# RWKV keys first with one norm chain and one block order for both heads, and an inverse with aligned diagonal blocks, in a two-layer hybrid decoder trunk

## The chip, the cores and the metric

The kernel runs on one core of a Trainium2 chip. The metric is the device time of one execution in microseconds, as the median of several runs. The engines are TensorE (matmuls, PE in the rows; its weight loads are PEld), VectorE (DVE), ScalarE (ACT), GpSimd (POOL) and the DMA queues (SP issues them).

## What is computed

Two layers, each on 512 tokens of width 1024, all in float32:

```python
h = rms_norm(x); p = h @ w_in             # columns for MLA, RWKV-7, Mamba-2 and three gates
x = x + (sum_i sigmoid(g_i) * (o_i @ W_br_i)) @ W_out
x = x + relu(rms_norm(x) @ W_1)**2 @ W_2
# the RWKV branch, 8 heads of 64:
p = p + (token_shift(p) - p) * mu;  r, k, v, xw, xa, xg = split(p)
decay = exp(-exp(-softplus(-(w0 + tanh(xw) @ w2)) - 0.5));  a = sigmoid(a0 + xa @ a2)
kk = k * k_k;  kk = kk / max(norm_per_head(kk), 1e-12);  k = k * (1 + (a - 1) * k_a)
state = state * decay + (state @ -kk) (kk * a)^T + v k^T;  y = state @ r     # per token
y = group_norm(y) + sum(r * k * r_k) * v;  o = y * (sigmoid(xg) @ g2)
```

The kernel computes the recurrence in 8 chunks of 64 tokens: within a chunk the delta rule becomes a triangular system, whose inverse is formed explicitly.

## The kernel before

Activations lie with features on the partitions: a tile of 128 x 512 holds two heads. A projection (`proj`, line 256 in `mm3`) is 24 matmuls of 128 x 512 (8 slices of the depth, three products of high and low parts); its weights are brought by DMA as `wraw`, rounded by ScalarE to `wH` (L222), and VectorE forms the rest `wL` (L223).

`rwkv_prep` loops over four blocks i of two heads each. For each it projects and mixes r, k (and v in layer 1; layer 2 has done v ahead with a residual) in `shifted` (L306, L358, L359). It forms the decay (`lw`, the scan at L437, `c`, `E1`), `a` (L450, L451), the squares `sq` and their sums per token and head `ss` (L454, L457), a reciprocal root by Newton steps on 8 columns (L200 to L208), a spread copy of it (L461), transposes to bring it back (`inv`, L464), and the normalised `kk` (L466). Then it writes the tiles `AR` (-kk and r, times decay; L471, L473) and `BK` (kk*a and k, over decay; L480, L481), each with an axis of two halves. The two heads of a tile, partitions 0 to 63 and 64 to 127, have these halves in opposite order, so each product is made in two pieces of 64 partitions, the second of most pairs on GpSimd. Then come the bonus `rk` (L484), its sum `bo` (L486), transposes of v (`vT`), and `N`, the 64 x 64 products of BK and AR for 8 chunks and two heads (L503), masked into `NA` (L505).

`rwkv_inverse` inverts 64 triangular blocks of 64 x 64 in `NA`. The two 32 x 32 diagonal blocks lie at columns 0 to 31 for the upper 32 rows and 32 to 63 for the lower, so the block transposes into `NT` (L627), back from `X` (L641) and into `T1` (L646) go over 32 partitions each, 4, 4 and 2 of them. Between them stand 31 steps of two VectorE operations (L635, L637). Small matmuls `Q` (L652) and `X12` (L661, the tile `X` in the rows) make the off-diagonal block.

`rwkv_chain` runs over the 8 chunks: `prepare` makes `A` (L545, both halves of BK against both of AR), the masked `CW` and `LT` (L549 to L563); then `RY` (L576), `U` (L585, with NA) and `YS` (L598) advance the state.

The stages are emitted with others interleaved (`mixer`): after blocks 2 and 3 of `rwkv_prep` (`PF`) and at the yields of the inverse and the chain (`FILL`) one step of MLA's projections or one gate projection is emitted. The source order is a priority only: when the program is built, a planner with estimated costs fixes the order on each engine and puts in the waits, so an engine can run later work earlier. Buffers limit it: two PSUM banks for projections, three of the tag `r`, eight SBUF tiles `pg`.

## Time and profile before

| what | us |
|---|---|
| median of 3 runs (2192.79 to 2195.28) | 2192.87 |
| the profiled execution | 2201.93 |
| its span, first to last instruction | 2199.8 |
| TensorE busy (mean granted clock 0.98) | 2114.2 |
| VectorE busy | 1421.7 |
| ScalarE busy | 911.9 |
| GpSimd busy | 359.8 |

The rows below come from the profiled execution. Busy time of TensorE is modelled, and its small matmuls overlap each other, so pace is read from a group of them. In the timeline a row can gather several instructions of a kind (xN); its time goes from the first one's start to the last one's end. A mean granted clock of 1.00 is 2.4 GHz, 0.50 is 1.2 GHz. The key stages lie at about 36 to 147 us (layer 1) and 1115 to 1248 us (layer 2), the inverses behind them to about 223 and 1322 us.

### The profile page before, as it was taken

Reading aid. Unit: us, or ns where it says so; the run is one execution under the profiler, and the core shown is the slowest. Engines: PE = TensorE matmul, PEld = TensorE weight load, DVE = VectorE, ACT = ScalarE, POOL = GpSimd, SP = SyncE. Lnnn points to the kernel's source line nnn. Section 1 sums busy time; section 2 is a strip of 40 time slices with the busy share of each in tenths; the row PEclk is TensorE's granted clock in tenths of the full one; section 3 lists DMA queues with packets and bytes.
Section 4 is the critical chain, followed back from the end, with each engine's and each line's share of the span. In section 5 each row is a group of like instructions: output and inputs, shape, how many; then the busy total and the mean of one; then the engine's idle time right before and its main releaser. Section 6 shows DMA issues by size and latency. Waiting matters only on the chain. (4 is left out here: it accounts for less than half of the span.)

```text
span 2199.8 us, 29935 instructions
## 1 busy us (share of the span) xinstructions
PE 2114.2 (96%) x11592; PEld 1672.0 (76%) x11592; DVE 1421.7 (65%) x2394; ACT 911.9 (41%) x1568; POOL 359.8 (16%) x258
## 2 busy tenths in 40 slices
PE   7998999999999999999998889999999999999999
PEld 6667767667778888888876677676677788888887
DVE  7988777977756543443569978779777554444433
ACT  5343433764423443333433434337644234433332
POOL 1120020111322111111021200202113121111110
PEclk9998999999999999999999979999999999999999
DMA  5332233114364233333432222331143642333232
GB/s 193 91 95 69 71 113 127 44 58 148 125 216 134 89 106 96 96 96 96 139 98 77 82 70 74 108 124 42 65 146 121 217 133 87 105 96 96 96 96 96
DMA packets 95613, 232.61 MB, mean 106 GB/s; under 512 B 17744, under 2 KB 27088, under 8 KB 95472
## 3 DMA queue, kind: packets, MB, share of 16 engines
q1 hardware_dynamic: 95472, 230.71, 33.0%
q8 instruction: 91, 1.49, 0.3%
q14 instruction: 50, 0.41, 0.1%
HBM read 197.64 MB, written 33.03 MB: 105 GB/s over the span
## 5 line engine op out<-in xcount | busy, mean ns | idle before, releaser
L256 PE MATMUL pj<-hH,wH 128*128 128x512 f32 (+1 forms) x1536 | 616.8, 402 | 8.4 <-ACT hH L225 8.4
L256 PE MATMUL pj<-hH,wL 128*128 128x512 f32 (+1 forms) x1536 | 616.7, 401 | 0.9 <-DVE wL L223 0.9
L256 PE MATMUL pj<-hL,wH 128*128 128x512 f32 (+1 forms) x1536 | 615.5, 401 | 0.1
L222 ACT CAST wH<-wraw 128x1024 fp32r<-128x1024 f32 (+1 forms) x314 | 327.6, 1043 | 654.4 <-PE pj L256 317.9
L223 DVE TENSOR_TENSOR wL<-wraw,wH 128x1024 fp32r<-128x1024 f32 (+1 forms) x314 | 415.2, 1324 | 140.1 <-ACT wH L222 139.6
L256 PEld LDWEIGHTS pj<-hH,wH 128*128 128x128 f32 (+1 forms) x1536 | 292.1, 190 | 75.2 <-ACT hH L225 8.4
L256 PEld LDWEIGHTS pj<-hH,wL 128*128 128x128 f32 (+1 forms) x1536 | 291.2, 190 | 65.7 <-issue 4.0
L256 PEld LDWEIGHTS pj<-hL,wH 128*128 128x128 f32 (+1 forms) x1536 | 291.9, 190 | 63.8 <-issue 2.5
L256 PE MATMUL pf<-uH,wH 128*128 128x512 f32 x512 | 199.2, 389 | 0.0
L256 PE MATMUL pf<-uL,wH 128*128 128x512 f32 x512 | 199.2, 389 | 0.0
L256 PE MATMUL pf<-uH,wL 128*128 128x512 f32 x512 | 199.2, 389 | 0.0
L324 POOL TENSOR_TENSOR u<-u,rsb 128x512 f32<-128x512 f32 x64 | 111.3, 1741 | 496.4 <-ACT u L323 474.7
L339 DVE TENSOR_TENSOR x<-x,pf 128x512 f32<-128x512 f32 x128 | 88.1, 688 | 139.0 <-PE pf L256 136.9
L223 DVE TENSOR_TENSOR uL<-u,uH 128x512 fp32r<-128x512 f32 x64 | 44.1, 692 | 138.1 <-ACT uH L222 138.1
L256 PEld LDWEIGHTS pf<-uH,wH 128*128 128x128 f32 x512 | 96.1, 188 | 20.1
L256 PEld LDWEIGHTS pf<-uL,wH 128*128 128x128 f32 x512 | 96.1, 188 | 20.0
L256 PEld LDWEIGHTS pf<-uH,wL 128*128 128x128 f32 x512 | 96.1, 188 | 19.8
L977 POOL TENSOR_TENSOR E<-E,CB 128x1280 f32<-128x1280 f32 x16 | 49.4, 3088 | 377.3 <-ACT E L974 333.6
L256 PE MATMUL br<-oH,wH 128*128 128x512 f32 x256 | 102.9, 403 | 6.3 <-ACT oH L222 6.3
L256 PE MATMUL br<-oL,wH 128*128 128x512 f32 x256 | 103.2, 403 | 3.0 <-DVE oL L223 3.0
L256 PE MATMUL br<-oH,wL 128*128 128x512 f32 x256 | 102.3, 400 | 0.0
L326 ACT ACTIVATE u<-u 128x512 f32<-128x512 f32 x64 | 40.5, 633 | 118.9 <-POOL u L324 118.9
(363 smaller groups left out, 2972.4 us busy)
## 6 DMA issues: line engine op xcount, KB each, us to landing
wraw<-in_w SPq DMA_DIRECT2D x302, 512.0 KB, 3.6
gd<-gt SPq DMA_DIRECT2D x48, 256.0 KB, 2.1
th<-gd SPq DMA_DIRECT2D x16, 512.0 KB, 3.9
xd<-x SPq DMA_DIRECT2D x8, 512.0 KB, 5.2
o_ssm<-ys SPq DMA_DIRECT2D x16, 256.0 KB, 2.1
x<-xd SPq DMA_DIRECT2D x8, 512.0 KB, 5.9
of<-o_ssm SPq DMA_DIRECT2D x16, 256.0 KB, 4.4
t<-gd SPq DMA_DIRECT2D x16, 256.0 KB, 2.7
```

What stands on the lines that cost most here:

```text
L222: nc.scalar.copy(out=H, in_=src)
L223: nc.vector.tensor_tensor(out=Lo, in0=src, in1=H.bitcast(F32), op=ALU.subtract)
L256: nc.tensor.matmul(out=ps, lhsT=ww if w_is_lhs else aa, rhs=aa if w_is_lhs else ww, start=first and k == 0 and q == 0, stop=last and k == ...
L324: nc.gpsimd.tensor_tensor(out=u, in0=u, in1=self.rsb, op=ALU.mult)
L326: nc.scalar.activation(out=u2, in_=u, func=AF.Square)
L339: nc.vector.tensor_tensor(out=xk, in0=xk, in1=ps, op=ALU.add)
L977: eng.tensor_tensor(out=e, in0=e, in1=CB[g], op=ALU.mult)
```

## The change

In `rwkv_prep` the four k blocks are projected first (`key`), straight into `BK[:, i, :, 1, :]`, and their sums of squares share one PSUM bank; one reciprocal root on 32 columns serves all. The decay of block i + 1 (`decay`) is emitted within block i. r is projected straight into `AR[:, i, :, 1, :]`. The spread copy of the root moves to ScalarE. Both heads have the same order of halves, so each product of AR and BK is one VectorE operation on 128 partitions, and GpSimd has none; the halving in `a` is folded into the factors. `pg` has 6 tiles for 8, `c` and `E1` have two each for one.
`N` is formed in 32-wide pieces, so that each diagonal block of 32 x 32 lies at columns 0 to 31 of its own rows: in `rwkv_inverse` one transpose of 128 partitions stands for each group of 4 or 2. Then the lower diagonal blocks are copied to columns 32 to 63 by ScalarE and their old place is cleared by GpSimd. `A` is formed in pieces of 64 x 64, with the halves reversed for the second head, so that CW has the order it had; `LT` takes three copies for two. Layer 1's norm projects block 4 ahead in place of block 0. The scaled parameters `dv[:, 26:30]`, `dv[:, 40:48]` and the paddings are changed to suit.

```diff
-        pg = lambda name: tp.tile([P, S], F32, name=name, tag="pg", bufs=8)
+        pg = lambda name: tp.tile([P, S], F32, name=name, tag="pg", bufs=6)
...
+            for d in range(2):
+                p = slice(64 * hp + 32 * d, 64 * hp + 32 * d + 32)
+                nc.gpsimd.affine_select(out=self.mst[p, 0, 0:32], in_=self.mst[p, 0, 0:32], pattern=[[1, 32]],
+                                        compare_op=ALU.is_gt, fill=0.0, base=0, channel_multiplier=-1)
+            nc.vector.memset(self.mst[64 * hp + 32:64 * hp + 64, 0, 32:64], 0.0)
+            for t, q, strict in ((self.msk, 1 - hp, True), (self.msk, hp, False)):
                 nc.gpsimd.affine_select(out=t[h, q, :], in_=t[h, q, :], pattern=[[1, 64]],
...
@@ -355,14 +364,15 @@
         st = self.sh[self.shn % 2]
         self.shn += 1
         self.scaled(st[:, 3:S + 3], ps)
-        nc.scalar.activation(out=out, in_=st[:, 3:S + 3], func=AF.Identity, scale=self.dv[:, j:j + 1])
-        nc.vector.scalar_tensor_tensor(out=out, in0=st[:, 2:S + 2], scalar=self.pc("rwkv_mu", j), in1=out, op0=ALU.mult,
-                                       op1=ALU.add)
+        v = (lambda t: t) if len(out.shape) == 2 else lambda t: t.rearrange("p (c t) -> p c t", c=8)
+        nc.scalar.activation(out=out, in_=v(st[:, 3:S + 3]), func=AF.Identity, scale=self.dv[:, j:j + 1])
+        nc.vector.scalar_tensor_tensor(out=out, in0=v(st[:, 2:S + 2]), scalar=self.pc("rwkv_mu", j), in1=out,
+                                       op0=ALU.mult, op1=ALU.add)
 
...
-        for i in range(4):
-            r, k = pg("r"), pg("k")
-            self.shifted(i, r)
+        pss = PS("ss")
+        def key(i):
+            k = BK[:, i, :, 1, :]
             self.shifted(4 + i, k)
-            if l == 0:
-                v = T("v", [P, S], 4)
-                self.shifted(8 + i, v)
-                nc.sync.dma_start(out=self.vfirst[i], in_=v)
-            else:
-                v = vs[i]
+            sq = pg("sq")
+            nc.scalar.activation(out=v8(sq), in_=k, func=AF.Square, scale=self.pc("rwkv_k_k", i))
+            for q in range(NC4):
+                nc.tensor.matmul(out=pss[:, 8 * i + 2 * q:8 * i + 2 * q + 2], lhsT=sq[:, q * P:(q + 1) * P],
+                                 rhs=self.bones[:, 0:P:64], start=True, stop=True)
+        def decay(i):
 
             ps = PS("lw")
             nc.tensor.matmul(out=ps, lhsT=self.wa2[0:64, i * P:(i + 1) * P], rhs=xwa[0:64], start=True, stop=True)
@@ -431,9 +444,11 @@
             nc.tensor.matmul(out=pa, lhsT=self.wa2[64:128, i * P:(i + 1) * P], rhs=xwa[64:128], start=True, stop=True)
             t = lw[:, :, 1:65]
             nc.scalar.activation(out=t, in_=v8(ps), func=AF.Tanh, scale=0.5, bias=self.dv[:, 14 + i:15 + i])
+            th = pg("a")
+            nc.scalar.activation(out=th, in_=pa, func=AF.Tanh, scale=0.5, bias=self.dv[:, 18 + i:19 + i])
             nc.vector.tensor_scalar(out=t, in0=t, scalar1=-0.5 * INV_SQRT_E,
                                     scalar2=-0.5 * INV_SQRT_E, op0=ALU.mult, op1=ALU.add)
-            c = T("c", [P, 8, 65])
+            c = T("c", [P, 8, 65], 2)
             nc.vector.tensor_tensor_scan(out=fl(c), data0=fl(scanm), data1=fl(lw), initial=0.0, op0=ALU.mult,
                                          op1=ALU.add)
             m = T("m", [P, 8], 2)
@@ -442,49 +457,54 @@
                                     op=ALU.subtract)
             nc.vector.tensor_tensor(out=f[:, i, 0:7], in0=c[:, 0:7, 64], in1=m[:, 1:8], op=ALU.add)
             nc.scalar.activation(out=f[:, i, 0:7], in_=f[:, i, 0:7], func=AF.Exp)
-            E1 = T("E1", [P, 8, 65])
+            E1 = T("E1", [P, 8, 65], 2)
             nc.scalar.activation(out=E1, in_=c, func=AF.Exp)
             nc.scalar.activation(out=c, in_=c, func=AF.Exp, scale=-1.0)
-            a = pg("a")
-            nc.scalar.activation(out=a, in_=pa, func=AF.Tanh, scale=0.5, bias=self.dv[:, 18 + i:19 + i])
-            nc.vector.tensor_scalar(out=a, in0=a, scalar1=0.5, scalar2=0.5, op0=ALU.mult, op1=ALU.add)
-            sq = pg("sq")
-            nc.scalar.activation(out=sq, in_=k, func=AF.Square, scale=self.pc("rwkv_k_k", i))
-            ps = PS("ss")
-            for q in range(NC4):
-                nc.tensor.matmul(out=ps[:, 2 * q:2 * q + 2], lhsT=sq[:, q * P:(q + 1) * P], rhs=self.bones[:, 0:P:64],
-                                 start=True, stop=True)
-            inv = self.rsqrt(tp, ps[:, 0:8], [P, 8], 1.0, 0.0, "kk", lo=1e-24)
-            ib = sq
-            nc.vector.tensor_copy(out=v8(ib), in_=inv.rearrange("p (g o) -> p g o", o=1).to_broadcast([P, 8, 64]))
+            return th, c, E1
+        key(0)
+        key(1)
+        dec = decay(0)
+        key(2)
+        key(3)
+        inv = self.rsqrt(tp, pss[:, 0:32], [P, 32], 1.0, 0.0, "kk", lo=1e-24)
+        for i in range(4):
+            r, k = AR[:, i, :, 1, :], BK[:, i, :, 1, :]
+            self.shifted(i, r)
+            if l == 0:
+                v = T("v", [P, S], 4)
+                self.shifted(8 + i, v)
+                nc.sync.dma_start(out=self.vfirst[i], in_=v)
+            else:
+                v = vs[i]
+            th, c, E1 = dec
+            kk = pg("kk")
+            nc.scalar.copy(out=v8(kk), in_=inv[:, 8 * i:8 * i + 8].rearrange("p (g o) -> p g o", o=1).to_broadcast([P, 8, 64]))
             ps = PS("inv")
             for q in range(NC4):
-                nc.tensor.transpose(out=ps[:, q * P:(q + 1) * P], in_=ib[:, q * P:(q + 1) * P], identity=self.ident)
-            kk = sq
-            nc.vector.scalar_tensor_tensor(out=kk, in0=k, scalar=self.pc("rwkv_k_k", i), in1=ps, op0=ALU.mult,
+                nc.tensor.transpose(out=ps[:, q * P:(q + 1) * P], in_=kk[:, q * P:(q + 1) * P], identity=self.ident)
+            nc.vector.scalar_tensor_tensor(out=v8(kk), in0=k, scalar=self.dv[:, 44 + i:45 + i], in1=v8(ps), op0=ALU.mult,
                                            op1=ALU.mult)
 
-            for hp in range(2):
-                h, e = half(hp), nc.gpsimd if hp else nc.vector
-                nc.vector.scalar_tensor_tensor(out=AR[h, i, :, hp, :], in0=v8(kk)[h], scalar=-1.0, in1=E1[h, :, 0:64],
-                                               op0=ALU.mult, op1=ALU.mult)
-                e.tensor_tensor(out=AR[h, i, :, 1 - hp, :], in0=v8(r)[h], in1=E1[h, :, 1:65], op=ALU.mult)
-            nc.vector.tensor_tensor(out=kk, in0=kk, in1=a, op=ALU.mult)
-            nc.vector.tensor_scalar(out=a, in0=a, scalar1=self.pc("rwkv_k_a", i), scalar2=self.dv[:, 26 + i:27 + i],
+            nc.vector.scalar_tensor_tensor(out=AR[:, i, :, 0, :], in0=v8(kk), scalar=-2.0, in1=E1[:, :, 0:64],
+                                           op0=ALU.mult, op1=ALU.mult)
+            nc.vector.scalar_tensor_tensor(out=kk, in0=th, scalar=1.0, in1=kk, op0=ALU.add, op1=ALU.mult)
+            nc.vector.tensor_tensor(out=BK[:, i, :, 0, :], in0=v8(kk), in1=c[:, :, 1:65], op=ALU.mult)
+            nc.vector.tensor_scalar(out=th, in0=th, scalar1=self.dv[:, 40 + i:41 + i], scalar2=self.dv[:, 26 + i:27 + i],
                                     op0=ALU.mult, op1=ALU.add)
-            nc.vector.tensor_tensor(out=k, in0=k, in1=a, op=ALU.mult)
-            for hp in range(2):
-                h, e = half(hp), nc.gpsimd if hp else nc.vector
-                e.tensor_tensor(out=BK[h, i, :, hp, :], in0=v8(kk)[h], in1=c[h, :, 1:65], op=ALU.mult)
-                e.tensor_tensor(out=BK[h, i, :, 1 - hp, :], in0=v8(k)[h], in1=c[h, :, 1:65], op=ALU.mult)
-            rk = r
-            nc.vector.scalar_tensor_tensor(out=rk, in0=r, scalar=self.pc("rwkv_r_k", i), in1=k, op0=ALU.mult, op1=ALU.mult)
+            nc.vector.tensor_tensor(out=k, in0=k, in1=v8(th), op=ALU.mult)
+            rk = kk
+            nc.vector.scalar_tensor_tensor(out=v8(rk), in0=r, scalar=self.pc("rwkv_r_k", i), in1=k, op0=ALU.mult,
+                                           op1=ALU.mult)
+            nc.vector.tensor_tensor(out=r, in0=r, in1=E1[:, :, 1:65], op=ALU.mult)
+            nc.vector.tensor_tensor(out=k, in0=k, in1=c[:, :, 1:65], op=ALU.mult)
+            if i < 3:
+                dec = decay(i + 1)
             ps = PS("bo")
             nc.tensor.matmul(out=ps, lhsT=self.bones, rhs=rk, start=True, stop=True)
-            bo = r
+            bo = rk
             nc.vector.tensor_tensor(out=bo, in0=v, in1=ps, op=ALU.mult)
             for hp in range(2):
                 nc.sync.dma_start(out=self.bod[i - i % 2 + hp, half(i % 2)], in_=bo[half(hp)])
@@ -500,8 +520,11 @@
             ps = PS("N")
             for q in range(8):
                 for hp in range(2):
-                    nc.tensor.matmul(out=ps[half(hp), q * 64:q * 64 + 64], lhsT=BK[half(hp), i, q, hp, :],
-                                     rhs=AR[half(hp), i, q, hp, :], start=True, stop=True)
+                    for d in range(2):
+                        o = 64 * hp + 32 * d
+                        a = AR[half(hp), i, q, 0, :].rearrange("p (u t) -> p u t", u=2)
+                        nc.tensor.matmul(out=ps[o:o + 32, q * 64:q * 64 + 64], lhsT=BK[half(hp), i, q, 0, 32 * d:32 * d + 32],
+                                         rhs=a[:, ::-1] if d else a, start=True, stop=True)
             nc.vector.tensor_tensor(out=NA[:, 8 * i:8 * i + 8, :], in0=v8(ps), in1=self.mst.to_broadcast([P, 8, 64]),
                                     op=ALU.mult)
             yield i
@@ -542,11 +565,14 @@
             for i in range(4):
                 for hp in range(2):
                     h = half(hp)
-                    nc.tensor.matmul(out=pss[hp][:, i * P:(i + 1) * P], lhsT=BK[h, i, c].rearrange("p a t -> p (a t)"),
-                                     rhs=AR[h, i, c].rearrange("p a t -> p (a t)"), start=True, stop=True)
+                    rhs = AR[h, i, c, ::-1] if hp else AR[h, i, c].rearrange("p a t -> p (a t)")
+                    for a in range(2):
+                        nc.tensor.matmul(out=pss[hp][half(a), i * P:(i + 1) * P], lhsT=BK[h, i, c, 1 - a if hp else a, :],
+                                         rhs=rhs, start=True, stop=True)
             for hp in range(2):
                 h, o, ps = half(hp), half(1 - hp), pss[hp]
-                nc.scalar.copy(out=CW[h, hp], in_=AR[h, :, c].rearrange("p i a t -> p i (a t)"))
+                src = AR[h, :, c, ::-1] if hp else AR[h, :, c]
+                nc.scalar.copy(out=CW[h, hp].rearrange("p i (a t) -> p i a t", a=2), in_=src)
                 pv = ps.rearrange("p (i n) -> p i n", i=4)
                 mk = self.msk[o].rearrange("p (o a) t -> p o (a t)", o=1).to_broadcast([64, 4, P])
                 nc.vector.tensor_tensor(out=CW[o, hp], in0=pv[o], in1=mk, op=ALU.mult)
@@ -559,8 +585,9 @@
                     nc.tensor.transpose(out=pt[:, i * P:(i + 1) * P], in_=BK[:, i, c].rearrange("p a t -> p (a t)"),
                                         identity=self.ident)
                 pv = pt.rearrange("p (i n) -> p i n", i=4)
+                nc.scalar.copy(out=LT[:, 0, :, half(0)], in_=pv[:, :, half(0)])
                 for hp in range(2):
-                    nc.scalar.copy(out=LT[:, hp, :, half(hp)], in_=pv[:, :, half(hp)])
+                    nc.scalar.copy(out=LT[half(1 - hp), 1, :, half(1)], in_=pv[half(hp), :, half(1)])
 
         Sk = None
         prepare(0)
@@ -619,12 +646,11 @@
 
     def rwkv_inverse(self, p4, PS, NA):
 
         nc = self.nc
         b3 = lambda t: t.rearrange("p (s t) -> p s t", s=32)
-        blk = [(32 * d, slice(64 * hp + 32 * d, 64 * hp + 32 * d + 32)) for hp in range(2) for d in range(2)]
         NT, Xf, tmp = b3(p4("NT")), p4("X"), b3(p4("Xt"))
-        for d, p in blk:
-            nc.vector.transpose(out=NT[p], in_=NA[p, :, d:d + 32].rearrange("p b t -> p t b"))
+        nc.vector.transpose(out=NT, in_=NA[:, :, 0:32].rearrange("p b t -> p t b"))
         yield 2
         X = b3(Xf)
         nc.gpsimd.memset(Xf, 0.0)
@@ -637,13 +663,14 @@
             nc.vector.tensor_tensor(out=X[:, 0:t, t:32], in0=X[:, 0:t, t:32], in1=tt, op=ALU.add)
             if t % 8 == 0:
                 yield 1
-        for d, p in blk:
-            nc.vector.transpose(out=NA[p, :, d:d + 32].rearrange("p b t -> p t b"), in_=X[p].rearrange("p s t -> p t s"))
+        nc.vector.transpose(out=NA[:, :, 0:32].rearrange("p b t -> p t b"), in_=X.rearrange("p s t -> p t s"))
         yield 1
         T1, Q = b3(p4("T1")), b3(p4("Q"))
+        nc.vector.transpose(out=T1, in_=NA[:, :, 0:32])
         for hp in range(2):
-            s1 = slice(64 * hp, 64 * hp + 32)
-            nc.vector.transpose(out=T1[s1], in_=NA[s1, :, 0:32])
+            s2 = slice(64 * hp + 32, 64 * hp + 64)
+            nc.scalar.copy(out=NA[s2, :, 32:64], in_=NA[s2, :, 0:32])
+            nc.gpsimd.memset(NA[s2, :, 0:32], 0.0)
         for g in range(2):
             ps = PS("Q")
             for b in range(16):
...
```

## Rows read from the trace of the kernel before

**Rows 1.** The page's engines: busy us (share of the span) and instructions.

```profile
PE 2114.2 (96%) x11592; PEld 1672.0 (76%) x11592; DVE 1421.7 (65%) x2394; ACT 911.9 (41%) x1568; POOL 359.8 (16%) x258
```

**Rows 2.** Windows, engine busy us (instructions): plain projections, and the key stage.

```profile
825.00:850.00 25.00, 25.00 (x112) 20.67 (x112) 11.64 (x13) 9.87 (x14) 5.36 (x3) 1.00 0.30 88
1200.00:1225.00 25.00, 22.30 (x131) 16.55 (x130) 22.67 (x45) 8.86 (x15) 3.89 (x3) 1.00 0.31 93
```

**Rows 3.** TensorE's waits over the whole span: total us, times, longest us.

```profile
PE Q L652 <- DVE T L646: 10.1, 2, 5.2
...
PE bo L486 <- DVE r L484: 8.1, 6, 1.9
PE inv L464 <- DVE sq L461: 7.3, 7, 1.9
...
PE up L256 <- DVE cL L226: 5.1, 2, 2.6
...
PE ss L457 <- ACT sq L454: 2.9, 7, 1.6
```

**Rows 4.** VectorE's groups, 1150 to 1250 us: busy us, mean ns, idle before.

```profile
L223 DVE TENSOR_TENSOR wL<-wraw,wH 128x1024 fp32r<-128x1024 f32 (+1 forms) x11 | 12.7, 1153 | 0.2 <-ACT wH L222 0.2
L471 DVE SCALAR_TENSOR_TENSOR AR<-sq,E 64x512 f32<-64x512 f32 x8 | 5.5, 685 | 0.2
...
L437 DVE TENSOR_TENSOR_SCAN c<-scanm,lw 128x520 f32<-128x520 f32 x4 | 5.0, 1240 | 0.3
L484 DVE SCALAR_TENSOR_TENSOR r<-r,prm,k 128x512 f32<-128x512 f32 x4 | 4.9, 1229 | 0.0
L480 DVE TENSOR_TENSOR BK<-sq,c 64x512 f32<-64x512 f32 x4 | 4.7, 1182 | 0.0
...
L207 DVE TENSOR_TENSOR rskk<-rskk 128x8 f32<-128x8 f32 x12 | 3.7, 306 | 0.3
```

**Rows 5.** Timeline of VectorE and GpSimd in layer 1: start us, us, instruction.

```profile
59.08 1.68 DVE L480 TENSOR_TENSOR BK<-sq,c 64x512 f32<-64x512 f32 x1
...
58.73 1.49 POOL L480 TENSOR_TENSOR BK<-sq,c 64x512 f32<-64x512 f32 x1 [6.51 <-DVE sq L474]
```

**Rows 6.** Tile NA: duration ns min/median/max, first and last start us.

```profile
L505 DVE TENSOR_TENSOR NA<-N,mst x8: 683/692/692, 66.6 to 1246.4; 128x512 f32<-128x512 f32 x8
L627 DVE STREAM_TRANSPOSE NT<-NA x8: 1929/2000/2060, 148.5 to 1253.2; 32x1024 f32<-32x1024 f32 x8
L641 DVE STREAM_TRANSPOSE NA<-X x8: 2168/2270/2352, 198.3 to 1304.1; 32x1024 f32<-32x1024 f32 x8
...
L646 DVE STREAM_TRANSPOSE T<-NA x4: 1233/1234/1236, 207.5 to 1307.5; 32x1024 f32<-32x1024 f32 x4
```

**Rows 7.** Windows as in rows 2; the granted clock is third from the end.

```profile
208.00:224.00 16.00, 15.26 (x292) 11.97 (x294) 7.38 (x8) 6.67 (x11) 0.00 (x0) 0.57 0.27 85
...
180.00:190.00 10.00, 8.55 (x44) 8.15 (x45) 7.93 (x21) 2.45 (x5) 1.27 (x1) 0.66 0.18 54
1276.00:1288.00 12.00, 10.31 (x47) 9.77 (x48) 8.87 (x22) 3.08 (x7) 1.27 (x1) 0.57 0.13 45
1232.00:1240.00 8.00, 7.70 (x32) 6.20 (x33) 6.14 (x11) 1.04 (x1) 2.10 (x1) 0.57 0.07 8
```

**Rows 8.** Timeline of TensorE: start us, us, instruction, tile rows*columns, x records.

```profile
63.88 1.12 PE L486 MATMUL bo<-r,bones 128*128 128x512 f32 x2 [1.33 <-DVE r L484]
...
65.38 1.15 PE L503 MATMUL N<-AR,BK 64*64 64x64 f32 x32
...
222.23 0.40 PE L576 MATMUL RY<-Z,CW 128*64 128x64 f32 x6
222.56 1.19 PE L661 MATMUL X<-NA,Q 32*32 32x32 f32 x62
...
247.52 1.16 PE L545 MATMUL A<-AR,BK 64*128 64x128 f32 x16
...
249.20 0.98 PE L576 MATMUL RY<-Z,CW 128*64 128x64 f32 x26
```

More of the change, by code (lines that the diff above doesn't have):

```diff
@@ L98, in setup @@
             h = slice(64 * hp, 64 * hp + 64)
-            for t, q, strict in ((self.mst, 0, True), (self.msk, 1 - hp, True), (self.msk, hp, False)):
+            for d in range(2):
[4 more added lines that the diff above has]
+            for t, q, strict in ((self.msk, 1 - hp, True), (self.msk, hp, False)):
                 nc.gpsimd.affine_select(out=t[h, q, :], in_=t[h, q, :], pattern=[[1, 64]],
@@ L158, in load_params @@
         self.prm = prm
-        dv = self.par.tile([P, 40], F32, name="dv", tag="dv", bufs=1)
+        dv = self.par.tile([P, 56], F32, name="dv", tag="dv", bufs=1)
         self.dv = dv
@@ L171, in load_params @@
                                     scalar2=None, op0=ALU.mult)
-        nc.vector.tensor_scalar(out=dv[:, 26:30], in0=prm[:, cs["rwkv_k_a"]:cs["rwkv_k_a"] + 4], scalar1=-1.0,
+        nc.vector.tensor_scalar(out=dv[:, 26:30], in0=prm[:, cs["rwkv_k_a"]:cs["rwkv_k_a"] + 4], scalar1=-0.5,
                                 scalar2=1.0, op0=ALU.mult, op1=ALU.add)
+        for o, n in ((40, "rwkv_k_a"), (44, "rwkv_k_k")):
+            nc.vector.tensor_scalar(out=dv[:, o:o + 4], in0=prm[:, cs[n]:cs[n] + 4], scalar1=0.5, scalar2=None,
+                                    op0=ALU.mult)
         self.hg = prm[:, cs["q_rope_g"]:cs["q_rope_g"] + 64].rearrange("p (a d) -> p a d", a=2)
@@ L1117, in run @@
                 ns, npool = self.open("nm")
-                self.norm(x, "norm_mix_g", npool, first, [B_RW + j for j in ((12, 13, 8) if l else (12, 13, 0))])
+                self.norm(x, "norm_mix_g", npool, first, [B_RW + j for j in ((12, 13, 8) if l else (12, 13, 4))])
                 ns.close()
@@ L1138, in mixer @@
         mc_s, mcp = self.open("mc", "right")
-        self.pad(mqp, 736)
+        self.pad(mqp, 672)
         qT = mqp.tile([P, NC4, 768], F32, name="qT", tag="qT", bufs=1)
@@ L1192, in mixer @@
         self.gp = mgp
-        self.pad(mgp, 864)
+        self.pad(mgp, 800)
         m = mgp.tile([P, KD, S], F32, name="m", tag="m", bufs=1)
```

## The prediction

> **What bounds the kernel now.** I read the page's table of engines first: TensorE is busy for 2114.2 of 2199.8 us [rows 1]. No other engine comes near, so a time can only be won where TensorE stands still, does less, or runs at its lower clock. Next the windows. A stretch of plain projections shows TensorE busy for all of 25.00 us with 112 matmuls, so a matmul of 512 columns starts every 0.22 us and a projection of 24 takes 5.4 us. In the key stage (`rwkv_prep`), TensorE is busy for 22.30 us and VectorE for 22.67 us of 25 [rows 2]: both are nearly full, and each waits for the other in turn. The list of TensorE's waits tells for what: 10.1 us (2 times) for the last transposes of the inverse, 8.1 us for the bonus product `r`, 7.3 us for the spread norm `sq`, 5.1 us for the low half `cL` of an MLA projection (queued on VectorE between operations of the inverse), 2.9 us for the squares [rows 3]. Last the granted clock: it drops behind several of these waits. In 208 to 224 us, behind the wait for the transposes, its mean is 0.57; 0.66 and 0.57 behind the two waits for `cL`, 0.57 around one for the spread norm [rows 7]. The clock there is at the lower of its two levels, 1.2 GHz in place of 2.4, for most of the stretch, and busy time at 1.2 GHz is half lost. The second layer's wait for the transposes has the same pattern.
>
> **What the planner does.** The order on an engine is not the source order: `RY` of the chain started before `X` of the inverse, though it is emitted after it [rows 8]. So a matmul that follows its own producer in the source doesn't make TensorE stand still by itself; the planner puts other projections ahead. TensorE waits where an operation on the chip lasts longer than it was planned. That is how I read every wait in rows 3, and it decides what I expect of the order with keys first.
>
> **The parts.**
>
> *VectorE in the key stage.* From the groups of layer 2 (four blocks) [rows 4]: the two half-height `AR` products become one of full height: half of 5.5, 2.8 us less. That full height costs no more than half height is shown by 692 ns for 128x512 (`NA<-N,mst`) [rows 6] beside 685 ns for the 64x512 of `AR` [rows 4]. One chain of the norm with 32 columns in place of four with 8: for its dearest line three quarters of 3.7, 2.8 us less. `BK` and `rk` get longer while GpSimd works: the `BK` product took 1.68 us while GpSimd's lasted from 58.73 to 60.22 us [rows 5], against 0.69 us undisturbed. Without GpSimd's half, `BK` falls from 4.7 to 4 x 0.69 = 2.8 us (1.9 less) and `rk` from 4.9 to 4 x 0.73 (2.0 less). That is 9.5 us of VectorE's time in a layer from four groups alone, with further small ones (the halving of `a`, the spread copy, which goes to ScalarE) on top. ScalarE was the less busy engine and gets eight copies of some 0.6 us: I cost them at nothing; planned by themselves, with the norm ready long before, nothing waits for them but the first.
> What ends later than planned today (`r` behind GpSimd's lock, `sq` behind the norm chain) is what goes: 8.1 + 7.3 = 15.4 us of TensorE's waits. The new order will have its own misses, so I keep a third of them: **10 us gained**, bounds 0 and 15.4.
>
> *The inverse.* Four transposes of 2.00 us become one, four of 2.27 one, two of 1.23 one [rows 6]: 3 x 2.00 + 3 x 2.27 + 1.23 = 14.0 us of VectorE's queue in a layer, taking a transpose of 128 partitions to last as long as one of 32 (not shown for this operation; by the heights above). Two copies and two memsets of `NA` are added, on ScalarE and GpSimd, beside the transpose of `T1`; the first Q matmul needs neither, the X matmuls need the copies, U the memset. The waits of 10.1 us lie behind six of these transposes (4 x 2.27 + 2 x 1.23 = 11.5 us, then 2.27 + 1.23 = 3.5); a planning error in proportion leaves 3 us: **7 us gained**, bounds 0 and 10.1. For `cL`, which queues behind the first four, I take **3 us** of 5.1, bounds 0 and 5.1. TensorE has filling work enough when the chain starts earlier, since the gates that follow in the chain are emitted as before.
>
> *The clock.* The lost time is (1 - clock) x stretch: 0.43 x 16 = 6.9 us, twice with layer 2; 0.34 x 10 = 3.4; 0.43 x 12 = 5.2; 0.43 x 8 = 3.4 [rows 7]; together 25.8 us. With about half of the waits in front gone, I take half: **13 us gained**, bounds 0 and 25.8.
>
> *TensorE's own work.* `N` has 64 records for 32 in a block, `A` 32 for 16 in a chunk, with tiles of half the width. Before, `N` needs (1.15 - 0.22) / 31 = 30 ns for a record, `A` (1.16 - 0.27) / 15 = 59 ns, `RY` (0.98 - 0.22) / 25 = 30 ns, `X` (1.19 - 0.24) / 61 = 16 ns [rows 8] (the first record's own length, 0.22 to 0.27 us, is taken off). `RY` alternates two column halves on the same rows, `A` two row halves on the same columns, and both go at the faster pace. If all four quadrants run together, a record of half width costs half: nothing added. If just two do, `A` doubles: + 0.89 x 16 chunks = 14.2 us, and `N` + 0.93 x 8 blocks = 7.4 us. I take `A` at 0, for it combines what `RY` and `A` show singly, and `N` at **3 us lost**, since its records come near the 16 ns of `X`; bounds 0 and 21.6.
> `RY`'s weights are loaded for the column half that the matmul before doesn't use, on the same rows, without a gap in its pace of 30 ns [rows 8]. The Trainium skill ("TensorE: Matmul & The Clock Gate", Part 3: Packing small matmuls) says the contrary for this kind of order: a weight load overlaps a running matmul only when the row group differs. By that rule the new `A` and `N`, which issue the two column parts of one row group in succession, would pair badly; what it would give is rival B, and `RY`'s row speaks against it.
>
> *Other edits.* The masks, the scaled parameters and the padding touch no busy stretch: nothing. `pg` falls from 8 to 6 buffers, and one of three PSUM banks `r` is held by `pss` while the keys run; the projections of the keys cover that with 5.4 us each: nothing, and some 3 us (as the squares' waits of rows 3) if not.
>
> **Sum.** 10 + 7 + 3 + 13 - 3 = 30 us less. The profiled execution took 2201.9 us (span 2199.8): 2172. The median of the runs shown stands to it as 2192.87 to 2201.93, which gives **2163 us**. All gains and no cost: 15.4 + 10.1 + 5.1 + 25.8 = 56.4 less, 2137.
>
> **Rivals.**
> *B, quadrants run in pairs only.* 21.6 us for `A` and `N` in place of 3: 33 - 21.6 = 11 less, 2190 for the execution, **2182**. For it: no row shows four parts at once. Against: both pairs do run together.
> *C, keys first takes the cover away, slower.* Today a block has two projections on TensorE beside its VectorE work; afterwards all keys come first, and a block in layer 2 keeps one. VectorE's work for a block is then at most 1.2 (`wL`) + 1.4 (`sh`, mix) + 3.2 (decay: the scan of 1.24, two of 0.7, two small ones of 0.3) + 6.3 (nine products of 0.7) + 1.4 (bonus, mask) = 13.5 us, an estimate that puts every full-width operation without a row at 0.7 [rows 4, 6]. TensorE's is 5.4 + 1.15 (`N`) + 1.1 (`bo`) + some 2.5 (decay matmuls and transposes, an estimate at the pace of `bo`) = 10.2 [rows 2, 8]. If the planner brings no later projection forward, 3.3 us are missing in each of 8 blocks, 26 us, and the waits of that size were followed by a clock loss of 3.4 us or more [rows 7]: 27 us. Against the 15.4 us of today that is 11 + 27 more, less 21 won at the inverse (7 + 3 + 11 of its clock), and 3 for `N`: 20 us more, 2222, or **2213**. It decides once a block finds fewer than 3.3 us of foreign matmuls. Against it: the planner does bring later work forward [rows 8], and the MLA projections and gates are there to be brought.
> *D, given back.* TensorE's waits merely move: the chain of chunks or the attention behind it, both also short of slack on VectorE, wait anew as much as is won. About 0, **2193**.
>
> **How the numbers follow.** The forecast has 0.64 (2137 to 2182), B 0.15 (2176 to 2190), D 0.09, C 0.12. The range for 8 in 10 reaches from 2140 (nearly all gains; some 0.05 lies below) to 2197 (D with its scatter; C is left out). A measurement of this kernel tells about 0.2%, 4.4 us, from no change; the three runs shown lie 0.11% apart. Faster by more: 0.64 + most of B, 0.78. Within: the rest of B and most of D, 0.10. Slower: C, 0.12.
>
> **What would show it.** VectorE's busy time in a key-stage window falls from 22.7 to below 19 of 25 us while TensorE's rises above 23.5; `BK` and `rk` stand at 0.7 us each; the inverse has three transposes of 1.2 to 2.3 us; TensorE's wait for `T` falls below 2 us a layer and the clock behind it stays near 1.00; `A` keeps 1.2 us a chunk. Doubled `A` and `N` mean B. New waits of 2 us for `r`'s or `sq`'s successors in each block, with clock at half behind them, mean C. The forecast is wrong as well if a full-height transpose takes four times as long, which leaves the inverse where it is.

## The result and the profile after

The changed kernel takes 2157.59 us (median of 4 runs, 2152.58 to 2159.48), beside 2192.83 us before: a ratio of 0.9839, 95% interval 0.9821 to 0.9858, so 35 us less. The forecast was 30 us less (2163); the time lies inside the range. A second measurement gave 0.9821 (0.9801 to 0.9842).

The execution profiled after took 2155.9 us, with a span of 2154.0. That one of before took 2201.9, 9 us above its median, so the two profiles lie 46 us apart and the medians 35; the account below is one of profiles. First the page's line of engines (busy us, share of the span, instructions):

```profile
PE 2088.4 (97%) x12104; PEld 1654.7 (77%) x12104; DVE 1357.7 (63%) x2290; ACT 929.4 (43%) x1594; POOL 325.1 (15%) x240
```

Against [rows 1], TensorE is busy for 25.8 us less with 512 more instructions, and idle for 2154.0 - 2088.4 = 65.6 us in place of 2199.8 - 2114.2 = 85.6, 20.0 less. Together 45.8. The idle part is found in TensorE's waits (us in total, times, longest):

```profile
PE ss L436 <- ACT sq L434: 4.9, 3, 4.0
...
PE up L265 <- DVE cL L235: 4.3, 2, 2.2
...
PE bo L506 <- DVE f L458: 3.2, 3, 1.2
...
PE bo L506 <- DVE kk L499: 0.8, 1, 0.8
...
PE inv L486 <- ACT kk L483: 0.2, 1, 0.2
```

Beside [rows 3]: the wait for the last transposes is gone (10.1 to 0), those for the bonus and the spread norm fell from 15.4 to 3.2 + 0.8 + 0.2 = 4.2, that for `cL` from 5.1 to 4.3, and that for the squares rose from 2.9 to 4.9. The sum went from 33.5 to 13.4, 20.1 less, which is all of the idle part; among the other waits some grew and some shrank. The busy part is put down to the clock, since the work did not shrink and the mean granted clock of the span rose from 0.980 to 0.990. Windows, columns as in [rows 2]; the granted clock is third from the end:

```profile
50.00:75.00 25.00, 24.00 (x112) 18.57 (x112) 17.81 (x36) 10.43 (x16) 0.00 (x0) 1.00 0.29 95
...
1150.00:1175.00 25.00, 24.00 (x162) 16.33 (x160) 19.88 (x40) 10.89 (x16) 0.00 (x0) 1.00 0.24 71
1175.00:1200.00 25.00, 24.84 (x226) 18.36 (x226) 23.44 (x40) 12.07 (x20) 0.00 (x0) 1.00 0.29 86
174.00:182.00 8.00, 7.50 (x48) 6.74 (x48) 7.66 (x14) 3.69 (x7) 2.57 (x3) 0.57 0.07 30
1250.00:1258.00 8.00, 7.50 (x52) 7.00 (x52) 7.67 (x13) 3.56 (x7) 2.71 (x3) 0.57 0.09 34
1130.00:1138.00 8.00, 7.07 (x20) 4.69 (x20) 1.60 (x3) 2.49 (x3) 0.00 (x0) 0.57 0.20 66
```

In these windows of the key stage TensorE now works 24.0 to 24.8 of 25 us and VectorE 17.8 to 23.4. Three stretches of 8 us at 0.57 are left: behind the two waits for `cL` and behind the one of 4.0 us for the squares. They lose 3 x 0.43 x 8 = 10.3 us, where [rows 7] lost 25.8.

### The profile page after: what moved, and what is told of

Read it like the earlier page. It is cut to its first block, busy times and chain, and to the rows that moved or that the text cites. A ratio compares the mean times of both kernels' runs of the same rounds, so it can differ in the third digit from the quotient of the medians.

```text
span 2154.0 us, 30817 instructions
## 1 busy us (share of the span) xinstructions
PE 2088.4 (97%) x12104; PEld 1654.7 (77%) x12104; DVE 1357.7 (63%) x2290; ACT 929.4 (43%) x1594; POOL 325.1 (15%) x240
## 4 chain that ended last, share of the span: by engine, by line
PE 72%; DVE 11%; issue 3%; ACT 3%; DMA 2%; POOL 2%; SPq 0%; ACTq 0%; DVEq 0%; POOLq 0%
PE pj L265 34%; PE pf L265 16%; PE br L265 6%; PE wo L265 4%; PE up L265 2%; DVE wL L232 2%; PE y L1017 1%; PE sc L866 1%; PE YS L625 1%; DMA of<-o_ssm 1%; DVE cy L947 1%; PE pT L884 1%; DVE P L873 1%; DMA wraw<-in_w 1%; PE o L892 1%
## 5 line engine op out<-in xcount | busy, mean ns | idle before, releaser
L265 PEld LDWEIGHTS pf<-uH,wH 128*128 128x128 f32 x512 | 96.1, 188 | 19.9
L265 PEld LDWEIGHTS pf<-uL,wH 128*128 128x128 f32 x512 | 96.1, 188 | 19.9
```

The costliest lines, as they stand in the source:

```text
L265: nc.tensor.matmul(out=ps, lhsT=ww if w_is_lhs else aa, rhs=aa if w_is_lhs else ww, start=first and k == 0 and q == 0, stop=last and k == ...
```

## The experiments

The planner orders every edited kernel anew, so a run differs from the kernel that it is compared with in its order too, not in its edit alone.

**The two halves of the change, each alone.** The theory: the key stage and the inverse gain independently, so the parts add up to the whole. The rival: they share VectorE's queue, and one part alone loses what it won. `prep_only` has the new key stage, with the old `N` and the old ten transposes:

```diff
-                    for d in range(2):
-                        o = 64 * hp + 32 * d
...
+                    nc.tensor.matmul(out=ps[half(hp), q * 64:q * 64 + 64], lhsT=BK[half(hp), i, q, 0, :],
+                                     rhs=AR[half(hp), i, q, 0, :], start=True, stop=True)
...
-        nc.vector.transpose(out=NT, in_=NA[:, :, 0:32].rearrange("p b t -> p t b"))
+        for d, p in blk:
+            nc.vector.transpose(out=NT[p], in_=NA[p, :, d:d + 32].rearrange("p b t -> p t b"))
```

> The change without its inverse: keys first, one norm chain and one block order as in the kernel after, but N in whole 64 x 64 products and the inverse with its ten transposes as before. Theory (two parts that add up): the waits of TensorE for the bonus and the spread norm fall from 15.4 to about 4 us, those for the last transposes (10 us) and the clock loss behind them stay; 12 to 18 us less than before, about 2178. Rival (the key stage alone carries the gain, since an inverse that starts earlier is hidden anyway): 30 us less, about 2163. Rival (only the inverse counts): no change, 2193.

Measured: 2201.25 us, ratio 1.0025 (1.0016 to 1.0035): **5 us slower**. `inverse_only` is the kernel before with the aligned `N` and the three transposes:

```diff
-        for d, p in blk:
-            nc.vector.transpose(out=NT[p], in_=NA[p, :, d:d + 32].rearrange("p b t -> p t b"))
+        nc.vector.transpose(out=NT, in_=NA[:, :, 0:32].rearrange("p b t -> p t b"))
```

> The kernel before with the inverse of the change alone: N in 32-wide pieces, one transpose each way on 128 partitions, two copies and two memsets; keys, norms and block order as before. Theory: the waits for the transposes and most of the clock loss behind them go, 17 to 24 us less than before, about 2172; waits for bonus and spread norm stay at 15 us. Rival (the key stage alone carries it): no change, 2193.

Measured: 2179.49, ratio 0.9915 (0.9898 to 0.9932), 19 us faster. The parts add up to 13 us and the whole gives 35 to 39: 22 us and more come only when both are there, and the theory of two gains that add up falls. TensorE's waits in `prep_only`:

```profile
PE Q L671 <- DVE T L665: 20.5, 4, 9.9
PE A L562 <- DVE LT L572: 12.4, 2, 6.2
...
PE up L260 <- ACT kvT L768: 5.1, 4, 2.5
```

The bonus's waits did fall, to under 7 us, and the spread norm's are gone; but the wait for `T` doubled against [rows 3], from 10.1 to 20.5, and one of 12.4 for `LT` is new. VectorE's timeline there (start us, us, instruction) shows what these stand behind:

```profile
137.65 0.17 DVE L210 TENSOR_TENSOR rsc<-ryc 128x4 f32<-128x4 f32 x1
...
138.32 7.76 DVE L646 STREAM_TRANSPOSE NT<-NA 32x1024 f32<-32x1024 f32 x4
146.12 0.16 DVE L211 TENSOR_TENSOR rsc<-rsc 128x4 f32<-128x4 f32 x1
...
183.90 8.74 DVE L660 STREAM_TRANSPOSE NA<-X 32x1024 f32<-32x1024 f32 x4
192.68 2.50 DVE L665 STREAM_TRANSPOSE T<-NA 32x1024 f32<-32x1024 f32 x2
195.21 0.75 DVE L230 SCALAR_TENSOR_TENSOR cL<-pj,prm,cH 128x512 fp32r<-128x512 f32 x1
```

On VectorE nothing overtakes these blocks. The first, 7.8 us, lies in the middle of a chain of tiny operations (`rsc`, MLA's norm), whose next step starts at 146.12; the second, 11.3 us, ends at 195.18, and `cL` follows it. While they run TensorE uses up what it has. The clock behind the wait for `T` was 0.50 in 194 to 206 us. So a key stage that ends earlier met the same blocks with less left for TensorE to do. The first `Q` came 14.8 us earlier than before (193.96 for 208.74 us), yet the first `wo` projection of the layer stood at 701.9 for 702.3: all of it was given back in between.

**The quadrants.** Rival B at its own place: the kernel before with `A` and `N` in the smaller pieces.

```diff
-                    nc.tensor.matmul(out=pss[hp][:, i * P:(i + 1) * P], lhsT=BK[h, i, c].rearrange("p a t -> p (a t)"),
-                                     rhs=AR[h, i, c].rearrange("p a t -> p (a t)"), start=True, stop=True)
+                    for a in range(2):
+                        nc.tensor.matmul(out=pss[hp][half(a), i * P:(i + 1) * P], lhsT=BK[h, i, c, a, :],
+                                         rhs=AR[h, i, c].rearrange("p a t -> p (a t)"), start=True, stop=True)
```

> The kernel before with A formed in pieces of 64 x 64 and N in pieces of 64 x 32, nothing else: the added cost of twice as many small matmuls by itself. Theory (all four quadrants run together): A keeps 1.2 us a chunk and N 1.1 us a block, no change, 2193 within 4 us. Rival (they run in pairs): A 2.0 us and N 2.1 us, 14 to 22 us more, 2207 to 2215.

Measured: 2195.66, ratio 0.9995 (0.9986 to 1.0004). The pieces cost nothing that can be measured, and B falls. TensorE's timeline of the kernel after shows the pace:

```profile
75.78 1.10 PE L526 MATMUL N<-AR,BK 64*32 64x64 f32 x64
...
140.71 0.88 PE L570 MATMUL A<-AR,BK 64*64 64x128 f32 x22
```

`N`: (1.10 - 0.22) / 63 = 14 ns for a record, so twice the records take the time that they took [rows 8]. `A`: (0.88 - 0.27) / 21 = 29 ns, half of the 59 ns before.

**The transposes, within the new kernel.** If it is the long block on VectorE that ties the parts together, ten transposes put back into the kernel after must cost much of the gain.

```diff
-        nc.vector.transpose(out=NT, in_=NA[:, :, 0:32].rearrange("p b t -> p t b"))
+        blk = [slice(32 * j, 32 * j + 32) for j in range(4)]
+        for p in blk:
+            nc.vector.transpose(out=NT[p], in_=NA[p, :, 0:32].rearrange("p b t -> p t b"))
...
-        nc.vector.transpose(out=T1, in_=NA[:, :, 0:32])
+        for p in blk[::2]:
+            nc.vector.transpose(out=T1[p], in_=NA[p, :, 0:32])
```

> The kernel after with its three transposes of 128 partitions in an inverse made again in pieces of 32 partitions, 4, 4 and 2 of them: 14 us more of VectorE's queue in each layer, all else as after. Theory (it is the transposes' time that TensorE waited for): waits for T of 3 to 5 us a layer return with a low clock behind them, 10 to 20 us more than after, 2167 to 2177. Rival (the earlier start of the inverse leaves cover enough): 2158, as after.

Measured: 2177.68, ratio 0.9927 (0.9905 to 0.9948), **20 us slower than after**. Its waits, of which none of the three came to more than 2.1 us in the kernel after:

```profile
PE up L265 <- DVE krd L315: 7.5, 2, 3.8
...
PE Q L683 <- DVE T L673: 3.9, 2, 2.0
...
PE A L570 <- ACT LT L590: 3.0, 2, 1.5
```

The first is for a result that queues behind the first block, the second for the end of the second block; the third is for a copy on ScalarE. So the length of the transposes costs some 20 us here. It is not all: with the same ten transposes this kernel is still 16 us faster than the one before, and `prep_only` is slower than it by some 23 us, though the blocks are about as long (in layer 1 7.7 and 11.7 us here, 7.8 and 11.3 there). What differs is the work that TensorE has left while VectorE is in the second block (windows as above, first `prep_only`, then `many_transposes`):

```profile
184.00:194.00 10.00, 0.10 (x2) 0.04 (x2) 9.86 (x6) 0.00 (x0) 0.00 (x0) 0.61 0.00 0
```

```profile
187.00:197.00 10.00, 8.26 (x65) 7.69 (x64) 9.88 (x9) 3.90 (x7) 0.94 (x1) 0.83 0.11 43
```

TensorE works for 0.1 us there and for 8.3 here, on MLA's projections and an `A` that the planner has placed later. Why it orders them so can't be read from a trace.

**GpSimd's share of the products.** The kernel after, with products in halves of 64 partitions and three of the four second halves on GpSimd again:

```diff
-            nc.vector.tensor_tensor(out=BK[:, i, :, 0, :], in0=v8(kk), in1=c[:, :, 1:65], op=ALU.mult)
+            for hp in range(2):
+                h, e = half(hp), nc.gpsimd if hp else nc.vector
+                e.tensor_tensor(out=BK[h, i, :, 0, :], in0=v8(kk)[h], in1=c[h, :, 1:65], op=ALU.mult)
```

> The kernel after with the products of the key stage in two halves of 64 partitions again, the second half of three of the four on GpSimd as before. Theory (VectorE's operations lengthen beside GpSimd, and the doubled product costs VectorE 0.7 us a block): BK and rk last 1.2 us in the mean again, waits for the bonus return to 1.3 us a block; 5 to 12 us more than after. Rival (VectorE has slack enough in the key stage now): within 3 us of after.

Measured: 2167.77, ratio 0.9867 (0.9848 to 0.9886), beside the kernel after on the same chip at 2157.26: 10 us slower. VectorE's group in layer 2 (busy us, mean ns, idle before) and TensorE's waits say why:

```profile
L497 DVE TENSOR_TENSOR BK<-kk,c 64x512 f32<-64x512 f32 x4 | 5.2, 1297 | 0.0
```

```profile
PE bo L512 <- DVE f L458: 9.2, 5, 2.2
...
PE bo L512 <- DVE kk L503: 2.5, 3, 1.1
```

Half a `BK` product beside GpSimd takes 1.30 us, the whole alone 0.68 (below); the waits of `bo` rise from 3.2 + 0.8 = 4.0 to 9.2 + 2.5 = 11.7 us. The edit halves the `AR` product too, on VectorE alone, so the 10 us are the price of the halves and of GpSimd's share in them together.

**Keys first, and one norm.** The kernel after, with k projected in its own block and four norm chains of 8 columns:

```diff
-        key(0)
-        key(1)
-        dec = decay(0)
-        key(2)
-        key(3)
-        inv = self.rsqrt(tp, pss[:, 0:32], [P, 32], 1.0, 0.0, "kk", lo=1e-24)
         for i in range(4):
...
+            pss = key(i)
...
+            th, c, E1 = decay(i)
+            inv = self.rsqrt(tp, pss[:, 0:8], [P, 8], 1.0, 0.0, "kk", lo=1e-24)
```

> The kernel after with each k projected inside its block again and a norm chain of 8 columns for each block; one block order, no GpSimd, new inverse as after. Theory (the planner covers either order, but four short norm chains cost VectorE 6 us a layer and the spread norm comes late): waits for the spread norm of 0.5 to 1 us a block return, 3 to 10 us more than after. Rival (keys first is what makes the key stage short): 15 us more, near the 2177 that the inverse alone gives. Rival (the order costs as much as it gives, by the 4.0 us wait for the first squares in layer 2): same as after or 4 us less.

Measured: 2162.03, ratio 0.9825 (0.9804 to 0.9846), not to be told from the kernel after. The order wins a wait and loses one:

```profile
PE inv L482 <- ACT kk L479: 6.8, 8, 1.2
```

These 6.8 us, one small wait in each block, stand in place of the wait for the squares, of which 1.0 us is left in layer 2. The execution profiled here is the slowest of its five (2167.99).

**Where the squares' wait comes from.** In the kernel after, layer 2, it stands behind v's residual, as the timeline shows:

```profile
1125.33 1.61 POOL L418 TENSOR_TENSOR vf<-vf,sg 128x512 f32<-128x512 f32 x1
...
1126.97 0.69 DVE L419 TENSOR_TENSOR v<-v,vf 128x512 f32<-128x512 f32 x1 [1.18 <-POOL vf L418]
1127.58 0.68 DVE L315 TENSOR_TENSOR sh<-pj,rsb 128x512 f32<-128x512 f32 x1
```

VectorE stands still for 1.18 us on GpSimd, and the key's `sh` is queued behind it. `v_late` emits the residual behind the keys:

```diff
-            ps = PS("vl")
...
-                nc.vector.tensor_tensor(out=vs[i], in0=vs[i], in1=vf, op=ALU.add)
...
         key(3)
+        if l > 0:
+            ps = PS("vl")
...
+                nc.vector.tensor_tensor(out=vs[i], in0=vs[i], in1=vf, op=ALU.add)
```

> The kernel after with layer 2's value residual (products on GpSimd, sums on VectorE) emitted behind the four keys in place of ahead of them. Theory (the 4.0 us wait for the first squares comes from VectorE, which stands before the first mix of k until GpSimd has the last residual product): the wait falls below 1 us, the clock stays up behind it, 4 to 8 us less than after. Rival (the wait moves to the next place where the residual is late): same as after within 3 us.

Measured: 2157.99, ratio 0.9823 (0.9803 to 0.9843), the same. TensorE's waits from 1120 to 1200 us there:

```profile
PE bo L507 <- DVE f L442: 5.0, 3, 3.7
PE ss L420 <- ACT sq L418: 0.5, 1, 0.5
```

The wait of 4.0 us became one of 0.5, and one of 3.7 us appeared at the first block's bonus, behind the residual, which VectorE now does at 1147 to 1157 us. It moved.

**Is it cover that is missing?** A theory for `prep_only`: the gain is lost because TensorE has no other work while the transposes run. Then two more projection steps, emitted in the inverse behind the transposes back from `X` (its fifth yield), must bring it back. The same edit on all three kernels:

```diff
-FILL = [0, 1, 1, 1, 1, 1, 1] + 20 * [1]
+FILL = [0, 1, 1, 1, 3, 1, 1] + 20 * [1]
```

> prep_only (new key stage, old inverse) with two more steps of filling work emitted between the last transposes of the inverse and its first matmuls (FILL[4] = 3 for 1). Theory (the key stage does save time, but TensorE then stands for the ten transposes, which last longer than planned; with cover it keeps the saving): the wait for T falls from 20.5 to below 10 us, 8 to 20 us less than prep_only, about 2188. Rival (VectorE's queue to the first chunk is simply the bound, and cover only moves the wait into the chain): within 4 us of prep_only, 2201.

Measured: 2202.02, ratio 1.0033 (1.0021 to 1.0046), as `prep_only`. The wait for `T` is gone, but:

```profile
PE up L260 <- ACT kvT L768: 22.9, 4, 11.3
...
PE up L260 <- ACT csq L739: 6.3, 1, 6.3
```

The brought-forward projections need VectorE themselves (their norms), stand behind the same blocks, and wait longer.

> The kernel before with the same two steps of filling work emitted earlier, nothing else. Theory (the 10.1 us wait for T and the clock loss behind it are a matter of cover): the wait falls below 4 us, 8 to 15 us less than before, about 2185. Rival (cover moves the wait on): 2196, as before.

Measured: 2210.34, ratio 1.0069 (1.0054 to 1.0084), 15 us slower than before:

```profile
PE bo L486 <- DVE r L484: 11.1, 7, 3.0
...
PE YS L598 <- DVE Z L587: 6.6, 3, 3.1
```

> The kernel after with the same two steps of filling work emitted earlier. Theory (no wait for T is left to cover): within 4 us of after, 2158; a gain would say that the low clock at the inverse, 3.4 us a layer, goes with more cover.

Measured: 2178.57, ratio 0.9926 (0.9906 to 0.9946), some 20 us slower than after, with waits of 8.3 us for `Z` in the chain (1.3 in the kernel after) and 7.1 for `cL` (4.3). Cover is not free: as the waits for `Z` in both suggest, what was brought forward to the inverse is missing in the chain. That TensorE stands without work at the block is shown above; the theory that work brought forward makes up for it falls in all three.

**The last losses.** In the kernel after, the low clock inside the inverse follows the waits for `cL`. VectorE and GpSimd just there:

```profile
166.84 0.34 DVE L663 TENSOR_TENSOR X<-X,Xt 128x175 f32<-128x175 f32 x1
167.22 1.29 DVE L661 TENSOR_TENSOR Xt<-NT,X 128x156 f32<-128x156 f32 x1
168.54 0.32 DVE L663 TENSOR_TENSOR X<-X,Xt 128x156 f32<-128x156 f32 x1
...
166.94 1.39 POOL L749 TENSOR_TENSOR csq<-csq 128x512 f32<-128x512 f32 x1 [30.78 <-issue]
```

A step takes 1.29 us while GpSimd adds MLA's squares (`csq`); without it, in the run below, the same step takes 0.32. `csq_vector` puts these six sums on VectorE:

```diff
-                    nc.gpsimd.tensor_tensor(out=sq, in0=sq, in1=acc, op=ALU.add)
+                    nc.vector.tensor_tensor(out=sq, in0=sq, in1=acc, op=ALU.add)
```

> The kernel after with the sums of the MLA squares (L749, csq) on VectorE in place of GpSimd, three in each layer, two of which lie in the inverse. Theory (beside GpSimd's 1.3 us an inverse step of VectorE took 1.24 to 1.29 us in place of 0.18 to 0.32, some 1 us, while the sum costs VectorE 0.7 us itself and comes half a us earlier): the 2.2 us wait for cL and the low clock behind it shrink, 2 to 8 us less than after. Rival (the swap is even on VectorE, and the wait for cL has its cause in the order): within 3 us of after.

Measured: **2146.59** (2143.13 to 2148.54), ratio 0.9778 (0.9762 to 0.9793), 9 to 13 us below the kernel after by the ratios (0.9839 and 0.9821). It beats both kernels. The rows of the tile, of the wait and of the windows:

```profile
L749 DVE TENSOR_TENSOR csq<-csq x6: 685/692/693, 131.7 to 1240.2; 128x512 f32<-128x512 f32 x6
```

```profile
PE up L265 <- DVE cL L235: 2.5, 2, 1.3
```

```profile
174.00:182.00 8.00, 7.95 (x151) 7.40 (x153) 7.56 (x15) 5.83 (x10) 1.89 (x2) 1.00 0.01 2
1240.00:1248.00 8.00, 7.76 (x119) 7.17 (x120) 7.74 (x14) 4.39 (x8) 1.64 (x2) 1.00 0.15 56
1125.00:1133.00 8.00, 7.15 (x37) 5.08 (x38) 4.33 (x6) 3.88 (x6) 0.00 (x0) 1.00 0.36 119
```

VectorE does six more operations of 0.69 us, and its busy time over the span is the same to 1 us (1357.1 for 1357.7). The waits for `cL` fall from 2.2 to 1.3 us each, and behind them the clock holds at 1.00 (layer 2 runs 9.6 us earlier at this step, so its windows lie earlier): 1.8 us of waits and two stretches of 3.4 us less lost, 8.7 of the 11 us between the two profiled spans (2154.0 and 2143.0). The third stretch is at 1.00 as well, behind a squares' wait of 2.4 us in place of 4.0. That can't be put down to the sums, none of which runs near it: in the second profile of the kernel after, unchanged, this wait was 5.9 us.

```profile
PE ss L436 <- ACT sq L434: 7.1, 4, 5.9
```

The gain is more than the 2 to 8 us expected.

## Why the prediction was right, and where it was not

**The total** (30 less forecast, 35 measured) was right, and the account of the two profiles follows its steps. Term by term:

*Key stage*, 10 us: the two waits fell by 11.2. Of its signs, TensorE above 23.5 of 25 us came in all of the windows shown (24.0 to 24.8), though not at the end of the stage (22.8 in 86 to 111 us); VectorE below 19 came in one of them (17.8; 19.9 and 23.4 in the others). The groups that were sized came to the sizes given (layer 2, busy us, mean ns, idle before):

```profile
L499 DVE SCALAR_TENSOR_TENSOR kk<-AR,prm,BK 128x512 f32<-128x512 f32 x4 | 3.0, 746 | 0.0
...
L490 DVE SCALAR_TENSOR_TENSOR AR<-kk,E 128x512 f32<-128x512 f32 x4 | 2.8, 688 | 0.1
...
L493 DVE TENSOR_TENSOR BK<-kk,c 128x512 f32<-128x512 f32 x4 | 2.7, 684 | 0.0
...
L216 DVE TENSOR_TENSOR rskk<-rskk 128x32 f32<-128x32 f32 x3 | 0.6, 188 | 0.1
```

Against [rows 4], `AR` 5.5 to 2.8, `BK` 4.7 to 2.7, `rk` 4.9 to 3.0, and the norm's dearest line 3.7 to 0.6. VectorE's busy time fell by 64.0 us in all, of which the transposes are 28.

*The inverse*, 7 us: 10.1. The assumption that a transpose of 128 partitions lasts as long as one of 32 is now shown, beside [rows 6]:

```profile
L653 DVE STREAM_TRANSPOSE NT<-NA x2: 1982/2009/2036, 136.4 to 1212.5; 128x1024 f32<-128x1024 f32 x2
L666 DVE STREAM_TRANSPOSE NA<-X x2: 2208/2214/2219, 175.1 to 1251.2; 128x1024 f32<-128x1024 f32 x2
L669 DVE STREAM_TRANSPOSE T<-NA x2: 1222/1224/1226, 177.8 to 1253.9; 128x1024 f32<-128x1024 f32 x2
```

*`cL`*, 3 of 5.1 us: mis-sized, it gave 0.8. It was put down to the transposes it queued behind; what stretched VectorE's queue there in the kernel after was GpSimd's `csq`, as `csq_vector` shows.

*The squares*, 0: 2.0 us worse, and 4.2 worse in the second profile. The prediction had said that 5.4 us of projections cover them; in layer 2 one squaring is late for another reason, v's residual on GpSimd. `v_late` shows that curing it alone wins nothing.

*The clock*, 13 us: mis-sized for the two profiles. By [rows 7] and the windows above, 25.8 - 10.3 = 15.5 us; by the mean clock of the whole span (0.980 and 0.990) 44.0 - 21.5 = 22.5, which is near the 25.8 us that TensorE's busy time fell. The windows listed were not all the places where the clock had dropped. In the medians it is less. The execution profiled before had a mean clock of 0.980, while in the four later sets of runs the kernel before has 0.983 in the median three times and 0.981 once, which loses 0.017 x 2193 = 37 us and 0.019 x 2197 = 42. Against the 21.5 of the kernel after that is some 16 to 20 us, an estimate from clocks that are given to three places.

*`N` and `A`*, 3 us lost: 0, by pace and by `split_only`. The Trainium skill ("TensorE: Matmul & The Clock Gate", Part 3: Packing small matmuls) lets a weight load overlap a running matmul only where the row group differs; at 14 and 29 ns a record, with column parts of one row group in succession, no run here shows a cost of that, and the measurement decides.

*What the planner does.* [rows 8] show `RY` ahead of 62 matmuls of `X`, not of all of them: the trace has others of `X` from 214.84 us on. That the planner changes the order of the source stands.

*Rivals.* B fell (`split_only`). C fell: TensorE is busier in the key stage, not less. D, the waits that merely move, was given 0.09 for the whole change; it is false for the whole and true for a part in one order: `prep_only` is just that, with the chain's `LT`, the inverse's `T` and MLA's projections as the places where it is given back.

**The step that failed** is thus not the total but its attribution: "10 us" and a share of the clock for the key stage by itself. With the old inverse it costs 5 us in `prep_only`, while with the new placing of `N` and the ten transposes the kernel is 16 us faster than before (`many_transposes`). With the inverse shortened, it is worth 0.9915 to 0.9839 or 0.9821, 17 to 21 us, of which 10 are the products in halves with GpSimd's share (`gpsimd_back`) and none that can be measured is the order with keys first and the single norm (`keys_in_loop`), which the title of the change puts first. The other 7 to 11, of work moved to ScalarE, the folded factors and the rest, were not taken apart. That the total came so near is in part luck: by the terms above the two profiles lie 46 us apart where 30 were forecast, and the medians lie closer because the execution profiled before had lost more to the clock than most.

**Open:** why the planner leaves TensorE without work at the old transposes in `prep_only` and not in `many_transposes`; what sets the squares' wait, 4.0 and 5.9 us in two executions of the same kernel; and `pg` with eight buffers, which no run tries.

## What to carry to other kernels

Look for the longest uninterrupted block on an engine that feeds the bound one, and for what the bound engine has left to do while it runs: savings ahead of such a block can be given back at it (`prep_only`), though they need not be (`many_transposes`), so parts of a change tried singly need not add up. An elementwise operation that is moved to GpSimd "for free" is paid on VectorE by whatever runs beside it, so price it by the neighbours' durations. A wait of 2.2 us cost 3.4 us more in clock here, so look at the clock behind a wait before pricing it.

## What was not expected of the hardware

- The VectorE operations shown that ran beside one of GpSimd were stretched to about the length of GpSimd's, even a tiny one: 0.32 to 1.29 us beside GpSimd's 1.39. Giving VectorE six sums of 0.69 us that took GpSimd 1.28 left VectorE's busy time unchanged.
- A transpose of 128 x 1024 takes the time of one of 32 x 1024: 2.01, 2.21 and 1.22 us after, 2.00, 2.27 and 1.23 before [rows 6].
- The granted clock was 0.57 behind the waits of 2.2 us for `cL` in the kernel after and 1.00 behind those of 1.3 in `csq_vector`, at the same step of the inverse. The length of a wait alone does not tell it: behind the 2.4 us for the squares in `csq_vector` it was 1.00 too.
